# A hybrid retention and S5 layer on one Trainium2 core: S5 output loads on GpSimd's queue, grouped input statistics, and the first gate unit behind the chunk products

## The chip, the cores and the metric

The kernel runs on one core of one Trainium2 chip. Time is device time of one execution in microseconds (us), lower is better. The engines are named as the profile names them: PE (TensorE, matrix products), DVE (VectorE), ACT (ScalarE), POOL (GpSimd) and SP (SyncE, which here only issues DMAs). A DMA is issued by an engine's instruction stream and waits there for what it needs, so each of these streams is also a queue: a DMA that waits holds up all that is issued behind it on the same engine.

## What is computed

One layer of a hybrid backbone on 128 context tokens and 1024 latent tokens of width 1024, all in float32:

```
mod = silu(cond) @ w_ada + b_ada;  sh1, sc1, g1, sh2, sc2, g2 = split(mod)
h = norm(x) * (1 + sc1) + sh1
q, k, v, g, u = split(h @ w_in)
o = norm(retention(q, k, v)) * silu(g)            # 4 heads, both directions, chunks of 64
y = gelu(S5(u));  y = y * sigmoid(y @ w_glu + b_glu)   # 32 groups of 16 channels, 64 complex states
x = LN1(alpha * x + g1 * (concat(o, y) @ w_out))
f = relu(norm-modulated(x) @ w_ff1 + b_ff1)**2 @ w_ff2 + b_ff2
x = LN2(alpha * x + g2 * f)
```

The final retention and S5 states of the context tokens are outputs too.

## The kernel before

Tokens lie in 9 tiles of 128 rows (one of context, eight of latent tokens), taken in three groups of 384 (g = 0, 1, 2). An fp32 product is made of three matmuls on split operands (`mm3`, L206 to L210): `split` (L195) makes a high part on ACT or DVE (L200 or L198) and a low part on DVE or, with the mark "p", on POOL (L201). The program is one stream per engine, in the order in which the code emits it; all weights come through SP's queue with `ld`, a few loads and stores through POOL's queue with `gl`. Some 30 SBUF tiles are handed out in turn (`slot`, `rel`).

The order of the work around the change is this:

1. **Start.** The first round of modulation (`mod_begin(0)`, weights `wa`), the input normalisation `ln0` (L520) of the nine tiles, one tile at a time (statistics on DVE, a square root on ACT, the scaled copy on ACT, L523), and the S5 parameter tables: `params_a` (its last part on POOL, L404 to L417, and PE transposes, L421), `params_b` (powers, POOL, L438 to L443), `params_y` (POOL, L459 to L464).
2. **Products of the S5 input.** `make_h(g, k)` transposes a 128-column slice of the group on PE (L529), modulates it on ACT (L540) and splits it on DVE (L543); `products(g, k, k + 1)` then multiplies it with the first three S5 input columns (`u_split(0)` to `u_split(2)` are their splits). Group 2's normalisations are emitted among the steps of groups 0 and 1.
3. **Chunk products.** For each S5 column u, `s5_T1(u)` (DVE, L619 to L621) makes a table, `s5_W1(u)` transposes it (PE L635, copies on ACT L636), `load_X(u)` reads the column's inputs (SP, L602), and `s5_V(u)` multiplies (PE L649). Passes of input column 3 (`unit_g(3, g)`) and of column 4, the first gate (`unit_g(4, g)`), stand between them. A pass is 24 matmuls of 384 columns.
4. **Weave.** `weave` (L100, called in L1126) merges four tracks by costs that the code states: the other input columns (`units(5, 20)`), the scan and the tables for the outputs, a round of modulation, and `y_track(2)`, the S5 outputs of columns 0 and 1.
5. **Retention and the rest of S5.** `y_load(2)`, the heads' scores, `mod_more(2)` (modulation weights `wa`, SP, L259; products `pm`, PE L269), `s5_y(2)`, `y_load(3)`, `s5_y(3)`, then the gated unit (GLU), the output product and the feed-forward.

An S5 output u is `y_load(u)` and `s5_y(u)`: the load brings 3.3 MB from DRAM (KD in 8 pieces of 64 KB, X with 576 KB, and for each direction WD with 512 KB and SD with 576 KB) on SP's queue into three "vec" tiles, one "wide" tile and two held ones; PE makes 24 groups of products (`py`, L1102 to L1104), ACT the gelu, and POOL's queue stores the result to DRAM (YD, L1108) and reads it back in 8 pieces in another layout (yT, L1113). The next column's load goes into the same tiles, so it starts when this column's products are done, and its X waits for the store.

POOL also makes the query factors of the retention heads (`qf`, `qb`, L1182 and L1183), 128x1024 each.

Of the kernel before, what the change touches and what calls it, by code (L numbers as in the profile page):

```python
# [18 lines left out]
D = 1024  # L19
# [12 lines left out]
def kernel(  # L32
# [191 lines left out]
    xt = {}  # L224
# [204 lines left out]
    def params_b():  # L429
        e = PO.tensor_tensor  # L430

        def cmul(k0, k1, m):
            w = k1 - k0
            o0, o1 = Ar[:, k0:k1], Ai[:, k0:k1]
            x0, x1 = Ar[:, 1:1 + w], Ai[:, 1:1 + w]
            mr, mi = bc(Ar[:, m], 1, w), bc(Ai[:, m], 1, w)
            tv = tmpq.rearrange("p (k c) -> p k c", c=64)[:, 0:w]
            e(o0, x0, mr, MUL)  # L438
            e(tv, x1, mi, MUL)
            e(o0, o0, tv, SUB)  # L440
# [6 lines left out]
        cmul(5, 9, 4)  # L447

    def params_y():
# [397 lines left out]
    X4 = [load_X(u) for u in range(3)]
    u_load(4)
    run(back)
    unit_g(3, 0, evac_u(3))  # L850
    u_split(4, "p")
    s5_W1(0)
    run(s5_T1(1))
# [13 lines left out]
    unit_g(4, 1, evacs[4])  # L867
    load_outparams()
    s5_V(2, X4[2])
    s5_W1(3)  # L870
    unit_g(4, 2, evacs[4])
    u_split(5, "p")
    s5_V(3, X4[3])
    u_load(6)
    params_d()

    extra, UV = [0.0], 0
# [194 lines left out]
        return t  # L1072

    def y_load(u):
        if not late:
            s5s.close()
            late.append(late_s.enter_context(tc.tile_pool(name="late", bufs=1)))
        W3 = ltile()
        W3v = W3.rearrange("p (g x) -> p g x", g=8)
        for j in range(8):  # L1080
            ld(W3v[16 * j:16 * j + 16], KD[u, :, :, (7 - j) * 16:(7 - j) * 16 + 128].rearrange("g c x -> c g x"))
        X = hold(6) if u < NY else slot("yX")
        load_X(u, X)
        W2, SS = [], []
        for d in range(2):
            w, s = ltile(), ((hold(7) if u < NY else slot("yS")) if d == 0 else ltile(True))
            ld(w.rearrange("p (g n) -> p g n", g=8), WD[u, d].rearrange("p (g n) -> p g n", g=8)[:, :, 16 - 16 * d:144 - 16 * d])
            ld(s.rearrange("p (a n) -> p a n", a=2), SD[d, :, :, 4 * u:4 * u + 4].rearrange("p a q n -> p a (q n)"))
            W2.append(w.rearrange("p (g n) -> p g n", g=8))
            SS.append(s.rearrange("p (g n) -> p g n", g=8))  # L1090
            if d == 0:
                s0 = s
        YL[u] = W3v, X, W2, SS, s0

    def s5_y(u):
        W3v, X, W2, SS, s0 = YL.pop(u)
# [12 lines left out]
        if u >= NY:  # L1109
            rel(X, s0)  # L1110
# [52 lines left out]
    def ret_tok(h):  # L1163
        r = RS[h]
        qT, kT, vT = (qkv[h, w] for w in range(3))
        r["Sf"], r["Sb"], r["kb"] = slot("Sf"), slot("Sb"), slot("kb")
        ld(r["Sf"][:, 0:128], state_ret[0, 0, 0, h])
        ld(r["Sb"][:, 7 * P:8 * P], state_ret[0, 0, 1, h])
        kf, kb, vt = kT, r["kb"], vT
        for c0, c1 in batches:  # L1170
            n = (c1 - c0) * P
            pk, pv = ps("pk"), ps("pv")
            for c in range(c0, c1):
                PE.transpose(blk(pk, c - c0, c - c0 + 1), blk(kT, c, c + 1), ident)
# [5 lines left out]
        r["qf"] = hold(6 + h % 2)  # L1180
# [32 lines left out]
    def ret_out(h, now=True):  # L1213
# [531 lines left out]
```

## Time and profile before

| | us |
|---|---|
| median of 3 runs (lowest, highest) | 1504.29 (1502.57, 1504.37) |
| the profiled execution | 1499.46 |
| its span | 1497.2 |
| PE busy in the span | 1374.8 |
| DVE, ACT, POOL busy | 814.1, 599.6, 211.7 |

The profiled execution lies 4.8 us (0.3%) under the median of the runs, and 2.3 us of it lie outside the span. The profile gives for each engine what it did and what released it when it had waited; a busy PE counts as busy at either clock, so the granted clock is read beside it.

### The profile page before, as it was taken

What the parts mean: (1) busy time and instruction counts of PE and PEld (TensorE: products, weight loads), DVE (VectorE), ACT (ScalarE), POOL (GpSimd) and SP (SyncE); (2) the same over time, 40 slices, a digit from 0 to 9 for tenths busy, and PEclk for the clock granted to TensorE, in tenths of its full rate; (3) what the DMA queues carried; (4) which work ended last, traced back from release to release, by engine and by line L of the source; (5) the groups of instructions that cost most, each with busy time, mean ns of one, the idle gap of its engine ahead of it and who ended that gap; (6) DMA issues with size and microseconds to landing.
All of it is one profiled execution on the core that took longest, in us unless ns stands there. A gap on an engine that the chain in (4) does not pass through costs nothing.

```text
span 1497.2 us, 19638 instructions
## 1 busy us (share of the span) xinstructions
PE 1374.8 (92%) x7631; PEld 1233.0 (82%) x7631; DVE 814.1 (54%) x1486; ACT 599.6 (40%) x1001; POOL 211.7 (14%) x206
## 2 busy tenths in 40 slices
PE   5767999998658899999999999999999999999996
PEld 2557979998556788888999999989999999899995
DVE  7553689858315577676435443664544356543345
ACT  4453612122122463235444454444455444444451
POOL 3610000002141631253000010010001001000002
PEclk9888999999879989999999999999999999999998
DMA  9403561176578615138544334347443424734321
GB/s 319 107 1 123 167 223 59 43 192 189 153 213 246 199 47 181 64 122 261 198 132 152 118 110 138 108 135 239 143 126 111 128 98 141 253 114 140 115 83 43
DMA packets 194941, 214.62 MB, mean 143 GB/s; under 512 B 19800, under 2 KB 158752, under 8 KB 194336
## 3 DMA queue, kind: packets, MB, share of 16 engines
q1 hardware_dynamic: 186400, 197.99, 42.1%
q0 software_dynamic: 3504, 10.54, 2.4%
q10 hardware_dynamic: 4944, 4.83, 0.9%
q8 instruction: 60, 0.98, 0.3%
q14 instruction: 33, 0.27, 0.1%
HBM read 186.31 MB, written 27.02 MB: 142 GB/s over the span
## 4 chain that ended last, share of the span: by engine, by line
PE 71%; DVE 10%; DMA 6%; issue 5%; ACT 3%; SPq 3%; POOL 1%; POOLq 0%; ACTq 0%; DVEq 0%
PE ff L210 8%; PE ff L208 8%; PE ff L209 8%; PE acc L1575 8%; PE acc L1574 8%; PE acc L1573 8%; PE pu L208 4%; PE pu L209 3%; PE pu L210 3%; PE op L1427 2%; PE op L1426 2%; PE op L1428 2%; PE pv L649 1%; DMA w1r<-in_w_ff_dram 1%; PE pm L269 1%
## 5 line engine op out<-in xcount | busy, mean ns | idle before, releaser
L208 PE MATMUL ff<-h,wh 128*128 128x384 f32 x768 | 258.9, 337 | 0.0
L210 PE MATMUL ff<-h,wl 128*128 128x384 f32 x768 | 257.8, 336 | 0.7 <-DVE wl L201 0.7
L209 PE MATMUL ff<-h,wh 128*128 128x384 f32 x768 | 257.3, 335 | 0.0
L201 DVE TENSOR_TENSOR hid<-r,hid 128x384 fp32r<-128x384 f32 x96 | 67.5, 704 | 342.7 <-ACT hid L200 342.2
L1575 PE MATMUL acc<-wh,hid 128*128 128x512 f32 x564 | 222.4, 394 | 5.5 <-DVE hid L201 5.5
L1574 PE MATMUL acc<-wl,hid 128*128 128x512 f32 x564 | 221.7, 393 | 0.0
L1573 PE MATMUL acc<-wh,hid 128*128 128x512 f32 x564 | 220.1, 390 | 0.4 <-ACT hid L200 0.3
L1551 ACT ACTIVATE r<-ff,bf 128x384 f32<-128x384 f32 x96 | 55.6, 579 | 306.1 <-PE ff L210 306.0
L208 PE MATMUL pu<-hTh,wh 128*128 128x384 f32 x480 | 168.8, 352 | 1.9 <-DVE hTh L542 1.2
L209 PE MATMUL pu<-hTl,wh 128*128 128x384 f32 x480 | 165.5, 345 | 3.4 <-DVE hTl L543 3.3
L210 PE MATMUL pu<-hTh,wl 128*128 128x384 f32 x480 | 164.0, 342 | 0.0
L201 DVE TENSOR_TENSOR wl<-w1r,wh 128x1024 fp32r<-128x1024 f32 x96 | 117.5, 1224 | 60.7 <-ACT wh L200 56.1
L208 PEld LDWEIGHTS ff<-h,wh 128*128 128x128 f32 x768 | 144.2, 188 | 3.3 <-ACT wh L200 0.4
L209 PEld LDWEIGHTS ff<-h,wh 128*128 128x128 f32 x768 | 144.2, 188 | 2.9
L210 PEld LDWEIGHTS ff<-h,wl 128*128 128x128 f32 x768 | 144.1, 188 | 1.0 <-DVE wl L201 1.0
L1575 PEld LDWEIGHTS acc<-wh,hid 128*128 128x128 f32 x564 | 106.1, 188 | 29.5 <-DVE hid L201 7.2
L1573 PEld LDWEIGHTS acc<-wh,hid 128*128 128x128 f32 x564 | 106.4, 189 | 21.0 <-ACT hid L200 1.0
L1574 PEld LDWEIGHTS acc<-wl,hid 128*128 128x128 f32 x564 | 106.2, 188 | 20.5
L201 DVE TENSOR_TENSOR wl<-w2r,wh 128x1024 fp32r<-128x1024 f32 x95 | 118.0, 1242 | 0.9 <-PE acc L1575 0.6
L200 ACT ACTIVATE wh<-w1r 128x1024 fp32r<-128x1024 f32 x96 | 100.5, 1047 | 26.9 <-DMA w1r<-in_w_ff_dram 26.4
L208 PEld LDWEIGHTS pu<-hTh,wh 128*128 128x128 f32 x480 | 92.9, 193 | 11.6 <-issue 6.9
L200 ACT ACTIVATE wh<-w2r 128x1024 fp32r<-128x1024 f32 x96 | 100.3, 1045 | 0.0
(445 smaller groups left out, 2087.3 us busy)
## 6 DMA issues: line engine op xcount, KB each, us to landing
w1r<-in_w_ff_dram SPq DMA_DIRECT2D x96, 512.0 KB
w2r<-in_w_ff_dram SPq DMA_DIRECT2D x96, 512.0 KB
wa<-in_w_ada_dram SPq DMA_DIRECT2D x48, 512.0 KB
wr<-in_w_in_dram SPq DMA_DIRECT2D x20, 512.0 KB
SD<-SB SPq DMA_DIRECT2D x8, 576.0 KB
WD<-W SPq DMA_DIRECT2D x8, 576.0 KB
RD<-xr POOLq DMA_DIRECT2D x9, 512.0 KB, 2.9
x<-RD SPq DMA_DIRECT2D x9, 512.0 KB
```

What stands on the lines that cost most here:

```text
L200: S.activation(hi, x, AF.Copy)
L201: (tt if leng == "v" else PO.tensor_tensor)(lo, x, hi.bitcast(F32), SUB)
L208: PE.matmul(out, lhsT=wh, rhs=xh, start=first, stop=False)
L209: PE.matmul(out, lhsT=wh, rhs=xl, start=False, stop=False)
L210: PE.matmul(out, lhsT=wl, rhs=xh, start=False, stop=last)
L1426: PE.matmul(po[hf], lhsT=mh, rhs=wo[kt][0][:, cs], start=(kt == 0), stop=False)
L1427: PE.matmul(po[hf], lhsT=mh, rhs=wo[kt][1][:, cs], start=False, stop=False)
L1428: PE.matmul(po[hf], lhsT=ml, rhs=wo[kt][0][:, cs], start=False, stop=(kt == KT - 1))
L1551: S.activation(r, pu[:, 0:384], AF.Relu, bias=bf1[:, f:f + 1])
L1573: PE.matmul(o, lhsT=hh[:, 0, tk], rhs=wh[:, cs], start=(f == 0), stop=False)
L1574: PE.matmul(o, lhsT=hh[:, 0, tk], rhs=wl[:, cs], start=False, stop=False)
L1575: PE.matmul(o, lhsT=hh[:, 1, tk], rhs=wh[:, cs], start=False, stop=(f == NF - 1))
```

## The change

- The normalisation of x is made for three tiles at once: `ln0_stats(g)` takes the statistics of a group (the inverse root by iterations on DVE, for group 2 on POOL) and `ln0_norm(g)` the three scaled copies on ACT. They are emitted earlier than the single ones.
- The low parts of S5 columns 0 and 1 move from DVE to POOL; the last part of `params_a` is emitted behind them.
- `params_y` moves from POOL to DVE, in four pieces of three operations, emitted one by one among the later steps of the products, ahead of `s5_T1(0)`. Its sign change (B2) moves to POOL, into `params_b`.
- The chunk products are written in another order, with T1 and W1 of the next column further ahead of V, and without the first gate: `units(4, 20)` now has its three passes, in the weave.
- `y_load` issues on POOL's queue. `y_load(2)` is emitted at the end of the weave's track, behind `s5_y(1)`, and `y_load(3)`, into tiles of its own, ahead of the first head's scores.
- The query factors of heads 0 and 1 move from POOL to DVE.

```diff
-    def ln0(sl):
-        x = xt[sl][:, 0:D]
-        nb, rs = row_norm(x)
-        S.activation(x, x, AF.Identity, bias=nb[:, 0:1], scale=rs[:, 0:1])
+    def ln0_stats(g, eng=None):
+        mv, rs = row_stats([xt[sl] for sl in range(3 * g, 3 * g + 3)], eng)
+        lnp[g] = neg_mean(mv, rs, 3, eng), rs
+
+    def ln0_norm(g):
+        nb, rs = lnp.pop(g)
+        for i in range(3):
+            x = xt[3 * g + i][:, 0:D]
+            S.activation(x, x, AF.Identity, bias=nb[:, i:i + 1], scale=rs[:, i:i + 1])
...
-            e = PO.tensor_tensor
-            e(y1, B1, q_r, MUL)
-            e(tv, B2, q_i, MUL)
-            e(y1, y1, tv, ADD)
+            tt(y1, B1, q_r, MUL)
+            tt(tv, B2, q_i, MUL)
+            tt(y1, y1, tv, ADD)
+            yield
...
-    for sl in range(3):
-        ln0(sl)
-    next(pa)
-    u_split(0)
+    ln0_stats(0)
+    ln0_norm(0)
+    u_split(0, "p")
...
-    u_split(1)
+    u_split(1, "p")
     u_split(2, "p")
+    ln0_stats(1)
+    ln0_norm(1)
+    next(pa)
...
-    back = s5_T1(0)
+    back = chain(params_y(), s5_T1(0))
...
-        if (g, k) in ((0, 5), (0, 7), (1, 5)):
-            ln0(6 + ((0, 5), (0, 7), (1, 5)).index((g, k)))
-        if g == 2 and k < 4:
-            next(back)
+        if (g, k) == (0, 7):
+            ln0_norm(2)
+        if (g, k) == (1, 4):
+            u_split(3, "p")
+        if j >= 4:
+            next(back, None)
         products(g, k, k + 1)
...
-    unit_g(4, 0, evacs[4])
-    s5_V(1, X4[1])
+    load_outparams()
     s5_W1(2)
     run(s5_T1(3))
+    s5_V(1, X4[1])
+    X4.append(load_X(3))
+    u_split(4, "p")
...
+        own = u == 3
+        vt = (lambda: slot("yv")) if own else ltile
+        W3 = vt()
+        X = slot("yX") if own else hold(6)
...
-            ld(W3v[16 * j:16 * j + 16], KD[u, :, :, (7 - j) * 16:(7 - j) * 16 + 128].rearrange("g c x -> c g x"))
-        X = hold(6) if u < NY else slot("yX")
-        load_X(u, X)
+            gl(W3v[16 * j:16 * j + 16], KD[u, :, :, (7 - j) * 16:(7 - j) * 16 + 128].rearrange("g c x -> c g x"))
+        gl(X, XD[u].rearrange("j (c g) n -> (j c) (g n)", g=8))
...
-    weave(units(5, 20), chain(s5_scan(), spill(), s5_w2(), tables()), mod_round(2, 5.0, 5.0, 2), chain(s5_finish(), y_track(NY)))
+    weave(units(4, 20), chain(s5_scan(), spill(), s5_w2(), tables()), mod_round(2, 5.0, 5.0, 2), chain(s5_finish(), y_track()))
...
-        PO.tensor_tensor(v8(r["qf"]), v8(qT), bc(RT[:, h], 1, 8), MUL)
-        PO.tensor_tensor(v8(qT), v8(qT), bc(RT[:, 4 + h], 1, 8), MUL)
+        e(v8(r["qf"]), v8(qT), bc(RT[:, h], 1, 8), MUL)
+        e(v8(qT), v8(qT), bc(RT[:, 4 + h], 1, 8), MUL)
...
-    y_load(2)
+    y_load(3)
     ret_scores(0)
...
     s5_y(2)
-    y_load(3)
```

**PE's order in the chunk products.** A row is the place of an instruction in PE's stream, its line, operation, output and inputs; pu is the output of a pass of an input column, pw that of `s5_W1`, pv that of `s5_V`, and wh_636 and wh_749 hold column 3, wh_1067 and wh_1327 the first gate. Before:

```order
314 L210 MATMUL pu_1115<-hTh_698,wl_637 128x384
315 L649 MATMUL pv_1141<-X_1030,W_211_1071 64x144 x4
...
322 L649 MATMUL pv_1190<-X_1030,W_214_1084 64x144 x4
323 L208 MATMUL pu_1197<-hTh_350,wh_636 128x384
...
346 L210 MATMUL pu_1197<-hTh_698,wl_637 128x384
347 L635 MATMUL pw_1225<-ident_71,T_217_1097 128x128 x4
...
350 L635 MATMUL pw_1244<-ident_71,T_220_1106 128x128 x4
351 L208 MATMUL pu_1272<-hTh_350,wh_1067 128x384
...
374 L210 MATMUL pu_1272<-hTh_698,wl_1068 128x384
375 L649 MATMUL pv_1299<-X_1032,W_233_1224 64x144 x4
```

After:

```order
314 L210 MATMUL pu_1059<-hTh_677,wl_750 128x384
315 L644 MATMUL pw_1086<-ident_71,T_174_984 128x128 x4
...
342 L210 MATMUL pu_1129<-hTh_677,wl_750 128x384
343 L658 MATMUL pv_1156<-X_980,W_182_1031 64x144 x4
...
350 L658 MATMUL pv_1205<-X_980,W_185_1044 64x144 x4
351 L644 MATMUL pw_1226<-ident_71,T_197_1111 128x128 x4
...
354 L644 MATMUL pw_1245<-ident_71,T_200_1120 128x128 x4
355 L658 MATMUL pv_1269<-X_982,W_191_1085 64x144 x4
...
383 L658 MATMUL pv_1503<-X_1325,W_250_1441 64x144 x4
384 L507 MATMUL ps_1510<-ident_71,cst_1216 128x128
...
391 L508 MATMUL ps_1528<-ident_71,cst_1216 128x128
392 L208 MATMUL pu_1552<-hTh_319,wh_1327 128x384
```

V of column 0 stood behind the second pass of column 3 and one W1, with gate passes between the V's; now it stands behind the third pass and two W1, a W1 stands between two V's, and the gate's first pass follows the last of the chunk products.

**POOL's queue at the end of the weave.** late, ub, yv, yX and yS are tiles that `y_load` fills; YD and yT are the stores and the reads back of `s5_y`. Before:

```order
76 L974 DMA RTd<-qd_3390 8x128
77 L975 DMA RT_1677<-RTd 128x1024
78 L1108 DMA YD<-ub_396_2705 128x8x144
79 L1113 DMA yT_3549<-YD 16x8x144 x8
80 L1108 DMA YD<-ub_396_2705 128x8x144
81 L1113 DMA yT_3633<-YD 16x8x144 x8
82 L1132 DMA bgl_3642<-in_b_glu_dram 128x4x1
```

After:

```order
88 L1118 DMA YD<-ub_376_2700 128x8x144
89 L1122 DMA yT_3420<-YD 16x8x144 x8
90 L1092 DMA late_3429<-KD 16x8x128 x8
91 L1093 DMA ub_376_2700<-XD 128x1152
92 L1099 DMA late_3439<-WD 128x8x128
93 L1100 DMA ub_376_2700<-SD 128x2x576
94 L1099 DMA late_3442<-WD 128x8x128
95 L1100 DMA late_3443<-SD 128x2x576
...
97 L1122 DMA yT_3583<-YD 16x8x144 x8
98 L1092 DMA late_3592<-KD 16x8x128 x8
...
104 L1141 DMA bgl_3609<-in_b_glu_dram 128x4x1
105 L1092 DMA yv_3611<-KD 16x8x128 x8
```

The six kinds of load of a column now stand between the reads back of the column before (yT) and the column's own store (YD); column 2's load and column 3's, into tiles of its own, stand behind yT of column 1.

**SP's queue from the last input column on.** wr is a weight column, Sf and Sb the retention's first states, wa the modulation's weights. Before:

```order
96 L1081 DMA late_3558<-KD 16x8x128 x8
...
98 L1087 DMA late_3568<-WD 128x8x128
99 L1088 DMA ub_396_2705<-SD 128x2x576
...
102 L1081 DMA late_3644<-KD 16x8x128 x8
103 L602 DMA yX_3653<-XD 128x1152
104 L1087 DMA late_3655<-WD 128x8x128
...
108 L1167 DMA Sf_3679<-in_state_ret_dram 128x128
...
111 L1168 DMA Sb_3736<-in_state_ret_dram 128x128
112 L259 DMA wa_3776<-in_w_ada_dram 128x1024
113 L259 DMA wa_3778<-in_w_ada_dram 128x1024
```

After:

```order
88 L1048 DMA KD<-Kp_3098 16x2x240 x4
89 L314 DMA wr_3177<-in_w_in_dram 128x8x128
90 L1176 DMA Sf_3646<-in_state_ret_dram 128x128
91 L1177 DMA Sb_3647<-in_state_ret_dram 128x128
92 L1176 DMA Sf_3703<-in_state_ret_dram 128x128
93 L1177 DMA Sb_3704<-in_state_ret_dram 128x128
94 L259 DMA wa_3745<-in_w_ada_dram 128x1024
95 L259 DMA wa_3747<-in_w_ada_dram 128x1024
```

SP's queue goes from the last weight column to Sf, Sb and the modulation's weights, with no load of an S5 output ahead of them.

## Rows read from the trace of the kernel before

**Rows 1.** the page, part 4: shares of the span in the chain of waits, by engine.

```profile
PE 71%; DVE 10%; DMA 6%; issue 5%; ACT 3%; SPq 3%; POOL 1%; POOLq 0%; ACTq 0%; DVEq 0%
```

**Rows 2.** waits of PE, 0 to 180 us (released line <- releaser: total us, times, longest).

```profile
PE xt L529 <- ACT xb L523: 14.9, 4, 7.9
...
PE pv L649 <- ACT W L636: 7.9, 1, 7.9
PE xt L529 <- ACT hTh L540: 5.5, 1, 5.5
...
PE pu L209 <- DVE hTl L543: 3.3, 7, 1.1
```

**Rows 3.** waits of PE, 320 to 580 us.

```profile
PE pm L269 <- DMA wa<-in_w_ada_dram: 20.7, 2, 15.1
PE py L1103 <- DMA ub<-SD: 7.2, 1, 7.2
```

**Rows 4.** windows (length, busy time and count by engine, granted clock, DMA share, GB/s).

```profile
75.00:100.00 25.00, 11.48 (x45) 10.73 (x46) 10.46 (x28) 12.54 (x26) 4.25 (x4) 0.73 0.00 1
...
358.00:385.00 27.00, 27.00 (x154) 26.77 (x147) 22.76 (x91) 4.37 (x12) 2.33 (x6) 0.94 0.56 171
400.00:450.00 50.00, 24.24 (x159) 20.76 (x160) 4.78 (x13) 10.67 (x21) 16.57 (x17) 0.67 0.80 214
```

**Rows 5.** PE's timeline, 97 to 127 us (start, length, instruction, idle time before it).

```profile
97.15 0.52 PE L210 MATMUL pu<-hTh,wl 128*128 128x384 f32 x1
97.47 0.52 PE L208 MATMUL pu<-hTh,wh 128*128 128x384 f32 x1
...
126.49 0.33 PE L208 MATMUL pu<-hTh,wh 128*128 128x384 f32 x1
126.67 0.33 PE L209 MATMUL pu<-hTl,wh 128*128 128x384 f32 x1
```

**Rows 6.** DVE's timeline, 70 to 105 us.

```profile
71.58 1.53 DVE L543 TENSOR_TENSOR hTl<-h,hTh 128x384 fp32r<-128x384 f32 x1
...
103.67 0.56 DVE L543 TENSOR_TENSOR hTl<-h,hTh 128x384 fp32r<-128x384 f32 x1 [2.58 <-ACT hTh L540]
104.14 0.69 DVE L619 TENSOR_TENSOR T<-Ar,Y 128x512 f32<-128x512 f32 x1
```

**Rows 7.** POOL's timeline, 34 to 69 us.

```profile
34.60 3.80 POOL L201 TENSOR_TENSOR wl<-wr,wh 128x512 fp32r<-128x512 f32 x2 [2.04 <-ACT wh L200]
...
67.38 1.49 POOL L464 TENSOR_TENSOR Y<-Y,pY 128x512 f32<-128x512 f32 x1
```

**Rows 8.** PE's timeline, 390 to 452 us.

```profile
390.99 0.34 PE L209 MATMUL pu<-hTl,wh 128*128 128x384 f32 x1
...
394.81 0.34 PE L210 MATMUL pu<-hTh,wl 128*128 128x384 f32 x1
...
419.74 2.17 PE L1158 MATMUL psc<-qkv,qkv 128*128 128x128 f32 x18
...
450.19 0.41 PE L1102 MATMUL py<-yX,late 128*128 128x144 f32 x2
```

**Rows 9.** POOL's timeline, 378 to 402 us (issues of DMAs).

```profile
378.72 0.58 POOL L975 DMA_DIRECT2D RT<-RTd  x1 [4.67 <-DMA RTd<-qd]
392.06 0.93 POOL L1108 DMA_DIRECT2D YD<-ub  x1 [12.76 <-ACT ub L1106]
397.14 4.22 POOL L1113 DMA_DIRECT2D yT<-YD  x8 [4.15 <-DMA late<-KD]
```

**Rows 10.** DMA issues of POOL, 385 to 470 us (KB each, median us from issue to landing).

```profile
yT<-YD POOLq DMA_DIRECT2D x24, 72.0 KB, 7.2
YD<-ub POOLq DMA_DIRECT2D x2, 576.0 KB, 4.4
```

**Rows 11.** SP's queue, 419 to 442 us (issues of DMAs).

```profile
419.44 4.32 SPq L1081 DMA_DIRECT2D late<-KD  x8
...
433.14 8.86 SPq L259 DMA_DIRECT2D wa<-in_w_ada_dram  x6
```

More of the change, by code (lines that the diff above doesn't have):

```diff
@@ L447, in params_b @@
         cmul(5, 9, 4)
+        B2 = s5in["B"][0:64, 512:1024]
+        PO.tensor_scalar(B2, B2, -1.0, None, MUL)
     def params_y():
@@ L798 @@
         make_h(0, k)
-    u_split(1)
+    u_split(1, "p")
     u_split(2, "p")
+    ln0_stats(1)
+    ln0_norm(1)
+    next(pa)
     for u in range(NU):
         products(0, 0, 4, (u,))
-    for sl in range(3, 6):
-        ln0(sl)
+    make_h(1, 0)
+    make_h(1, 1)
     run(pa)
     params_b()
-    make_h(1, 0)
-    make_h(1, 1)
     products(1, 0, 1)
@@ L818 @@
     next(steps)
+    ln0_stats(2, PO)
     products(1, 2, 3)
@@ L821 @@
     del waA, waB
-    params_y()
-    u_split(3, "p")
     order = [(g, k) for g in range(2) for k in range(4, KT)] + [(2, k) for k in range(KT)]
@@ L833 @@
     products(1, 3, 4)
-    back = s5_T1(0)
+    back = chain(params_y(), s5_T1(0))
     for j, (g, k) in enumerate(order):
         ahead(j + 3)
-        if (g, k) in ((0, 5), (0, 7), (1, 5)):
-            ln0(6 + ((0, 5), (0, 7), (1, 5)).index((g, k)))
-        if g == 2 and k < 4:
-            next(back)
+        if (g, k) == (0, 7):
[4 more added lines that the diff above has]
+            next(back, None)
         products(g, k, k + 1)
+    run(back)
     for u in range(NU):
         rel(*uw[u])
+    u_load(4)
+    X4 = [load_X(u) for u in range(2)]
+    run(s5_T1(1))
+    unit_g(3, 0, evac_u(3))
+    s5_W1(0)
     SB = big("SB")[:, 0:64 * NCOL].rearrange("p (r d l n) -> p r d l n", r=2, d=2, l=16)
@@ L846 @@
     SE = SE_.rearrange("p (r d l s) -> p r d l s", r=2, d=2, l=16)
[L847 to L853, printed above, removed]
     unit_g(3, 1, evac_u(3))
-    s5_V(0, X4[0])
-    unit_g(3, 2, evac_u(3))
     s5_W1(1)
     run(s5_T1(2))
-    X4.append(load_X(3))
+    unit_g(3, 2, evac_u(3))
+    s5_V(0, X4[0])
+    X4.append(load_X(2))
     u_load(5)
-    unit_g(4, 0, evacs[4])
-    s5_V(1, X4[1])
+    load_outparams()
     s5_W1(2)
     run(s5_T1(3))
+    s5_V(1, X4[1])
+    X4.append(load_X(3))
+    u_split(4, "p")
     params_s()
     params_c()
-    unit_g(4, 1, evacs[4])
-    load_outparams()
     s5_V(2, X4[2])
     s5_W1(3)
-    unit_g(4, 2, evacs[4])
-    u_split(5, "p")
     s5_V(3, X4[3])
-    u_load(6)
     params_d()
@@ L1077, in y_load @@
             late.append(late_s.enter_context(tc.tile_pool(name="late", bufs=1)))
-        W3 = ltile()
-        W3v = W3.rearrange("p (g x) -> p g x", g=8)
+        own = u == 3
+        vt = (lambda: slot("yv")) if own else ltile
+        W3 = vt()
+        X = slot("yX") if own else hold(6)
+        tiles = [W3, X]
+        W3v = W3[:, 0:D].rearrange("p (g x) -> p g x", g=8)
         for j in range(8):
-            ld(W3v[16 * j:16 * j + 16], KD[u, :, :, (7 - j) * 16:(7 - j) * 16 + 128].rearrange("g c x -> c g x"))
-        X = hold(6) if u < NY else slot("yX")
-        load_X(u, X)
+            gl(W3v[16 * j:16 * j + 16], KD[u, :, :, (7 - j) * 16:(7 - j) * 16 + 128].rearrange("g c x -> c g x"))
+        gl(X, XD[u].rearrange("j (c g) n -> (j c) (g n)", g=8))
         W2, SS = [], []
         for d in range(2):
[L1086 to L1089, printed above, removed]
+            w, s = vt(), slot("yS") if own else hold(7) if d == 0 else ltile(True)
+            tiles += [w, s]
+            wv = w[:, 0:D].rearrange("p (g n) -> p g n", g=8)
+            gl(wv, WD[u, d].rearrange("p (g n) -> p g n", g=8)[:, :, 16 - 16 * d:144 - 16 * d])
+            gl(s.rearrange("p (a n) -> p a n", a=2), SD[d, :, :, 4 * u:4 * u + 4].rearrange("p a q n -> p a (q n)"))
+            W2.append(wv)
             SS.append(s.rearrange("p (g n) -> p g n", g=8))
-            if d == 0:
-                s0 = s
-        YL[u] = W3v, X, W2, SS, s0
+        YL[u] = W3v, X, W2, SS, tiles if own else []
     def s5_y(u):
-        W3v, X, W2, SS, s0 = YL.pop(u)
+        W3v, X, W2, SS, tiles = YL.pop(u)
         Xv = X.rearrange("p (g n) -> p g n", g=8)
@@ L1108, in s5_y @@
         gl(YD[u].rearrange("g p n -> p g n"), Xv)
-        if u >= NY:
-            rel(X, s0)
+        rel(*tiles)
         yt = ltile(True) if u == 3 else slot("yT")
@@ L1115, in s5_y, with y_track @@
         dump(f"yT{u}", yt)
-    def y_track(n):
-        for u in range(n):
+    def y_track():
+        for u in range(2):
             y_load(u)
-            yield YL1
+            yield 22.0
             s5_y(u)
             extra[0] += 5.5
-            yield YL2
-    YL1, YL2, NY = 22.0, 2.0, 2
-    weave(units(5, 20), chain(s5_scan(), spill(), s5_w2(), tables()), mod_round(2, 5.0, 5.0, 2), chain(s5_finish(), y_track(NY)))
+            yield 2.0
+        y_load(2)
+    weave(units(4, 20), chain(s5_scan(), spill(), s5_w2(), tables()), mod_round(2, 5.0, 5.0, 2), chain(s5_finish(), y_track()))
     rel(*hTh, *hTl)
@@ L1179, in ret_tok @@
             S.copy(blk(vt, c0, c1), pv[:, 0:n])
-        r["qf"] = hold(6 + h % 2)
+        r["qf"] = slot("qf") if h < 2 else hold(6 + h % 2)
+        e = tt if h < 2 else PO.tensor_tensor
         v8 = lambda z: z[:, 128:1152].rearrange("p (c i) -> p c i", c=8)
-        PO.tensor_tensor(v8(r["qf"]), v8(qT), bc(RT[:, h], 1, 8), MUL)
-        PO.tensor_tensor(v8(qT), v8(qT), bc(RT[:, 4 + h], 1, 8), MUL)
+        e(v8(r["qf"]), v8(qT), bc(RT[:, h], 1, 8), MUL)
+        e(v8(qT), v8(qT), bc(RT[:, 4 + h], 1, 8), MUL)
     def ret_kv(h):
@@ L1235, in ret_out @@
         if h < 2:
-            rel(qb, vt)
+            rel(qb, vt, qf)
         if now:
```

9 lines of the change are left out of this document (5 added, 4 removed).

## The prediction

> **What bounds the kernel now.** PE carries 71% of the chain of waits [rows 1], and the change leaves its matmuls as they are, so the time can fall only where PE stands idle or runs at the lower clock. I read the waits of PE next, in two stretches that hold what the diff touches. Up to 180 us [rows 2] the longest are transposes that wait for a normalised tile (14.9 us in four waits, the longest 7.9), a transpose behind ACT's hTh (5.5), V of column 0 behind W (7.9), and products behind the low part hTl (3.3 in seven). From 320 us on [rows 3] it is modulation products behind their weights (20.7 in two, the longest 15.1), and the S5 output products behind SD (7.2). The windows [rows 4] show what idling costs besides: from 75 to 100 us PE was busy for 11.5 of 25 us at a mean granted clock of 0.73, from 400 to 450 us for 24.2 of 50 at 0.67. At the upper level (2.4 GHz) matmuls follow each other every 0.17 to 0.18 us, at the lower (1.2 GHz), just after such a wait, every 0.32 [rows 5]. What follows 580 us is not touched and shifts as a whole.
>
> **Part 1, start and products of the S5 input.** Minus is faster.
>
> - The 7.9 and the 5.5 us [rows 2] come from one cause: group 2's tiles are normalised one by one, DVE, ACT, DVE, ACT, behind each other's queues. With the statistics of three tiles made before the group is due, both go: -13.4. The other three waits of that row (14.9 - 7.9 = 7.0) are for group 1's tiles, whose statistics also come earlier, but PE's L421 transposes and DVE's other work stand near; I take -1.5 (ends 0 and -7).
> - The hTl of 71.58 us took 1.53 us while POOL was still at `params_y` (1.49 an operation); alone it took 0.56 [rows 6, 7]. With those operations gone from POOL, the 3.3 us of hTl waits go: -3.
> - Added: `params_y` on DVE, 12 operations of the size and kind of T1's, 0.69 each [rows 6], three to a step, plus the step's hTl of 0.56: 2.6 us, where PE's step takes about 1.9 (estimate: nine matmuls at 0.174 and three transposes). Four steps make +2.9. `u_split(3)` on POOL then slows DVE once more, I take +2. Sum +5; ends 0 (DVE runs ahead by the steps buffered) and +10 (each of the eight steps slowed by POOL).
> - Two more low parts on POOL, 3.80 us each [rows 7]: they stand ahead of products that are not due for 5 us or more, and beside `params_a`, which nothing needs before the T1 tables. Nothing; without that cover up to 4, within the +10 above.
>
> **Part 2, chunk products.** The 7.9 us for W vanish, since in the new order V of column 0 stands behind two W1 and the third pass: -7.9. New tightness: W1 and V of the next columns follow each other without gate passes between, and column 2's X is loaded into a tile just freed. No row shows these waits; the nearest is the 7.9 for W itself, the other end is nothing. I take +4 (ends 0, +9). The three gate passes leave: the 22 intervals between the second and the last of a pass's 24 matmuls take 3.82 us (390.99 to 394.81 [rows 8]), so a pass takes 4.17 and three make -12.5 here.
>
> **The clock.** Behind each of the three long waits PE works at the lower level for a while. From the mean clock of 0.73, 13.5 of those 25 us were at the lower level [rows 4]; taking 4 us of work behind each wait, that costs 2 us each: -6 (ends -3, -8).
>
> Parts 1, 2 and the clock without the passes: -13.4 - 1.5 - 3 + 5 - 7.9 + 4 - 6 = -22.8 (ends about -30 and -12). The weave then begins 35 us earlier. By the order it has 38 passes up to its last chunk kernel (pK) in both kernels, the gate's three now at the head, and ten behind that place instead of seven; PE is full in it, so I let it shift unchanged. `params_s`, `params_c`, the query factors on DVE and the sign change on POOL stand beside that work: nothing; without cover 2 us.
>
> **Part 3, the S5 outputs.** Counted on before's clock, from the end of y(0)'s products (390.8, just ahead of the pass of [rows 8]). Before, the store is issued at 392.06 (0.93 us) and the eight reads back from 397.14 to 401.36 [rows 9]; y(1) ended at 419.74 and y(2) began at 450.19 [rows 8]. PE now has four passes there instead of one: 16.7 us, which take the place of waiting, so the 12.5 us moved are hidden if y(1) comes no earlier. y(1)'s loads now stand behind the eight reads back on POOL, and a queue lets no more than eight DMAs be under way: KD from 401.4 to 405.6 at the earliest, or 3 us later if each waits for a read back to land (7.2 us [rows 10]); then X, two WD (as the store, 0.93 each) and two SD (0.6 each, as RT's 0.58 [rows 9]): 3.7 us more, 409 to 412. Landing takes 4.4 (store) to 7.2 (reads back), and the modulation's weights share the engines: y(1) starts at 414 to 422, I take 422, and ends at 429.5, 10 us later than before.
>
> Between y(1) and y(2) PE had 15.3 us of work and 15.1 of waiting for weights (30.45 in all [rows 3, 8]). The weights leave SP 8.9 us of issues [rows 11] that stood behind column 2's load, issued from 419.44; now nothing holds them, so that wait goes. In its place y(2) waits for its own load: store at 430.5, reads back to 440, loads to 448 or 451, landed at 456: +6 against 450.2 (ends -5, where only PE's work counts, and +14). y(3)'s load, into its own tiles, follows at once, two heads' products ahead of its use: nothing; without that cover it would be what y(2) pays, 6. The second wait for weights (20.7 - 15.1 = 5.6) goes, as SP is no longer held up by column 3's load: -5.5 (ends 0 and -5.6).
>
> **Sum.** -22.8 - 12.5 + 6 - 5.5 = -34.8 on the profiled 1499.5: 1464.7. That execution lay 4.8 under its median; I add half of that, as the next one need not: **1467**. Own range of this case: 1457 to 1478.
>
> **The rivals.**
>
> 1. *Loads on POOL and weights on SP meet.* y(1)'s load (3.3 MB), column 0's reads back (0.6) and six modulation weights (3.1) now want the DMA engines from about 405 us on. At the 214 GB/s of the window 400 to 450 [rows 4] 7 MB take 33 us, so y(1) would start at 433 to 438 and y(2) at 464 to 470: 14 to 20 us instead of 6, and more if lanes also wait. Time 1476 to 1488, I take 1480. For it: that window's DMA share was 0.80 with PE half idle. Against: it is a mean over idle stretches. The Trainium skill ("DMA: Bandwidth & Descriptors", Issuing engines are not separate DMA queues) says that DMAs of all issuing engines run on the same 16 DMA engines, so another queue saves only issue time; by it the weights gain the 13.7 us of issues that stood ahead of them (419.44 to 433.14 [rows 11]) and no transfer gets shorter. No run here shows the two at once. Chance 0.2.
> 2. *The front stays bound.* DVE, with `params_y` and POOL's splits beside it, sets the pace in the products, and the chunk products wait for W: part 1 and 2 at their other end, -12. Time 1478, up to 1488 with a late y(1). Chance 0.08.
> 3. *Slower: a column's load takes much longer on POOL.* Its WD and KD are 512-byte pieces, 1024 in a WD. y(1) and y(2) have no time to spare, y(0) a little, which I leave out. If each load takes L longer, the loss is 3L, and it eats the 35 us from L = 12; at 20 us the time is 1467 + 60 = 1527. For it: the reads back, 72 KB each, took 7.2 us to land [rows 10]; no row shows such a load there. Against: the store of 1024 pieces took 0.93 us to issue and 4.4 to land, and RT's issue 0.58 us in a stretch where DVE was busy for 22.8 of 27 us [rows 4, 9]. The Trainium skill (same page, SWDGE vs HWDGE vs iDMA) says that GpSimd writes the descriptors of its DMAs into SBUF, from which some DVE work locks it out; RT's row does not show that. Chance 0.07.
> 4. *No change.* The shift of 23 us before the weave is waited for inside it (weight columns on SP), and y(2) costs what the passes gave. Time 1500 to 1506. Against: PE is full in the weave. Chance 0.04.
> 5. *Better.* Part 1 at its low end and y(2) as early as PE's work allows: 1450. Chance 0.03.
>
> **The numbers.** The forecast gets 0.58. A measurement here tells 0.2%, 3 us, from no change. Faster: 0.58 + 0.2 + 0.08 + 0.03 = 0.89; same 0.04; slower 0.07. The range reaches over rivals 1 and 2, 1457 to 1488, and leaves out 0.14 and the tails.
>
> **What would show it.** Right: no wait over 3 us of PE before the weave but the first ones, its beginning at 140 to 144 us; no wait for W; y(1) some 30 us behind y(0) with four passes in between, a wait of 8 to 14 us for SD or WD ahead of y(2), none for modulation weights. Wrong: T1 or hTl ahead of PE for more than 10 us, y loads that land over 15 us after their issue, or PE waiting inside the weave where before it did not.

## The result, and the profile after

The changed kernel takes 1464.55 us (median of 4 runs, 1460.46 to 1465.77) against 1503.43 (4 runs of the kernel before, same chip): ratio 0.9738, 95% interval 0.9716 to 0.976, so 38.9 us faster. The profiled execution took 1460.46 us, with a span of 1458.4, 38.8 less than before's.

Where the span went is read from the same events in both timelines of PE:

| event | before | after | difference | since the event above |
|---|---|---|---|---|
| first pass of the weave | 177.35 | 138.56 | -38.8 | -38.8 |
| first product of y(0) | 384.94 | 342.60 | -42.3 | -3.6 |
| first work behind y(1) | 419.74 | 384.44 | -35.3 | +7.0 |
| first work behind y(2) | 456.07 | 420.88 | -35.2 | +0.1 |
| first product of y(3) | 486.97 | 443.63 | -43.3 | -8.1 |
| end of the span | 1497.2 | 1458.4 | -38.8 | +4.5 |

The waits of PE up to 180 us, to be held against [rows 2]:

```profile
PE xt L538 <- ACT xb L532: 5.4, 3, 3.9
...
PE pu L209 <- DVE hTl L552: 3.0, 3, 2.2
PE pu L208 <- ACT hTh L549: 1.8, 1, 1.8
```

The three waits for group 1's tiles are still there (14.9 less 7.9 was 7.0, now 5.4); those for a tile of group 2 (7.9), for hTh (5.5) and for W (7.9) are gone. Two windows show what is left, the products of groups 1 and 2, and the chunk products:

```profile
75.00:100.00 25.00, 21.80 (x105) 20.18 (x106) 20.04 (x34) 15.21 (x24) 3.02 (x2) 0.80 0.00 1
105.00:138.50 33.50, 33.36 (x379) 31.75 (x378) 24.92 (x71) 25.35 (x88) 2.58 (x1) 1.00 0.71 206
```

In the first PE is busy for 21.8 of 25 us, where it was busy for 11.5 [rows 4], still at a mean clock of 0.80; in the second it works for 33.36 of 33.50 us at the full clock, so the chunk products in their new order have no wait left. The timeline of PE from y(0) to y(2) (the last field is the idle time before a row and what ended it):

```profile
368.15 0.48 PE L1112 MATMUL py<-ub,late 128*128 128x144 f32 x2 [2.87 <-issue]
371.28 0.82 PE L1113 MATMUL py<-ub,late 128*128 128x144 f32 x2 [2.64 <-DMA ub<-SD]
377.60 0.82 PE L1114 MATMUL py<-late,late 128*128 128x144 f32 x2 [5.50 <-DMA late<-SD]
...
384.44 2.17 PE L1167 MATMUL psc<-qkv,qkv 128*128 128x128 f32 x18
...
405.01 0.82 PE L1112 MATMUL py<-ub,late 128*128 128x144 f32 x2 [7.70 <-DMA ub<-XD]
408.37 0.82 PE L1113 MATMUL py<-ub,late 128*128 128x144 f32 x2 [2.54 <-DMA ub<-SD]
412.98 0.82 PE L1114 MATMUL py<-late,late 128*128 128x144 f32 x2 [3.79 <-DMA late<-SD]
```

y(1) has waited 2.9 + 2.6 + 5.5 = 11.0 us and y(2) 7.7 + 2.5 + 3.8 = 14.0, both for loads (for the 2.9 the profile names no releaser; X, issued at 362.71, landed in 5.0 us in the median, which is about then); no wait of the modulation products is among the rows from 280 us on. That list has a new one, for the query factors of head 2:

```profile
PE py L1114 <- DMA late<-SD: 9.3, 2, 5.5
PE py L1112 <- DMA ub<-XD: 7.7, 1, 7.7
PE po L1236 <- POOL ub L1192: 5.3, 1, 5.3
...
PE po L1237 <- POOL ub L1193: 1.6, 1, 1.6
```

POOL's queue shows what stands ahead of the loads and of the factors (issues of DMAs, with the idle time before them):

```profile
349.72 0.92 POOL L1118 DMA_DIRECT2D YD<-ub  x1 [11.46 <-ACT ub L1116]
354.33 4.22 POOL L1122 DMA_DIRECT2D yT<-YD  x8 [3.69 <-DMA YD<-ub]
358.54 4.18 POOL L1092 DMA_DIRECT2D late<-KD  x8
...
365.79 0.71 POOL L1100 DMA_DIRECT2D late<-SD  x1
...
461.71 4.21 POOL L1122 DMA_DIRECT2D late<-YD  x8 [9.96 <-DMA YD<-yX]
465.94 2.35 POOL L1192 TENSOR_TENSOR ub<-ub,RT 128x1024 f32<-128x1024 f32 x1
```

The load of column 1 is issued behind the eight reads back of column 0: its last part at 365.79, 16.1 us behind the store at 349.72. The eight reads back of column 3 wait 10 us for their store to land, and the factors for head 2, next on POOL, come only at 465.94. In the kernel before, these factors stood behind the same reads back, but the reads back waited 3.7 us:

```profile
494.15 0.93 POOL L1108 DMA_DIRECT2D YD<-yX  x1 [3.63 <-ACT yX L1106]
498.76 4.21 POOL L1113 DMA_DIRECT2D late<-YD  x8 [3.68 <-DMA YD<-yX]
502.99 2.40 POOL L1182 TENSOR_TENSOR ub<-ub,RT 128x1024 f32<-128x1024 f32 x1
```

What differs is the traffic beside the store. Before, SP's next load (the gate, GD) waited for that store to land:

```profile
SPq L1217 <- DMA YD<-yX: 9.3, 1, 9.3
```

In the changed kernel, where column 3's load has other tiles, this wait is gone: SP issues the gate at 450.10 and three loads of 512 KB up to 451.46, beside the store of 450.82. From 451 to 456 us the DMA engines moved 319 GB/s, against 135 before between the store and its landing (494.5 to 499).

### The profile page after: what moved, and what is told of

It is laid out like the page before. It is cut to its first block, busy times and chain, and to the rows that moved or that the text cites. A ratio compares the mean times of both kernels' runs of the same rounds, so it can differ in the third digit from the quotient of the medians.

```text
span 1458.4 us, 19628 instructions
## 1 busy us (share of the span) xinstructions
PE 1367.7 (94%) x7631; PEld 1230.0 (84%) x7631; DVE 809.2 (55%) x1473; ACT 595.0 (41%) x990; POOL 227.4 (16%) x260
## 4 chain that ended last, share of the span: by engine, by line
PE 50%; DVE 9%; issue 3%; ACT 3%; DMA 2%; POOL 1%; POOLq 0%; SPq 0%; DVEq 0%; ACTq 0%
PE ff L210 8%; PE ff L208 8%; PE ff L209 8%; PE acc L1584 8%; PE acc L1583 8%; PE acc L1582 8%; DMA w1r<-in_w_ff_dram 1%; DVE xr L1449 1%; DVE st L157 1%; DVE op L1448 1%; DVE st L158 1%; DVE o L1627 1%; DVE hid L201 1%; ACT xr L1454 1%; DMA RD<-xr 0%
## 5 line engine op out<-in xcount | busy, mean ns | idle before, releaser
L1582 PEld LDWEIGHTS acc<-wh,hid 128*128 128x128 f32 x564 | 106.4, 189 | 21.8 <-ACT hid L200 1.8
```

The costliest lines, as they stand in the source:

```text
L1582: PE.matmul(o, lhsT=hh[:, 0, tk], rhs=wh[:, cs], start=(f == 0), stop=False)
```

## The experiments

Each is compared with the kernel before by its ratio; a difference of ratios times 1500 us gives the distance from the changed kernel (0.9738). With the intervals of both ratios its bounds are about 4 us.

| run | edit of the changed kernel | median | ratio (95%) | against the change, us |
|---|---|---|---|---|
| e1 | loads of S5 outputs on SP | 1472.98 | 0.9799 (0.9783 to 0.9814) | +9 |
| e2 | first gate among the chunk products | 1491.26 | 0.9919 (0.9902 to 0.9935) | +27 |
| e3 | group 2 normalised tile by tile | 1473.45 | 0.9807 (0.9792 to 0.9821) | +10 |
| e4 | reads back behind the next load | 1449.47 | 0.9646 (0.9628 to 0.9664) | -14 |
| e5 | all query factors on DVE | 1454.53 | 0.9691 (0.9677 to 0.9706) | -7 |
| e6 | temporary of `params_y` in its own tile | 1465.2 | 0.9762 (0.9748 to 0.9775) | +4 |
| e7 | e4, e5 and e6 together | 1438.84 | 0.9588 (0.957 to 0.9605) | -22 |
| e8 | `params_y` on POOL | 1458.87 | 0.9712 (0.9696 to 0.9727) | -4 |
| e9 | before, with the S5 output part alone | 1509.94 | 1.0053 (1.0039 to 1.0067) | |
| e10 | e7 and two more | 1437.31 | 0.9576 (0.9559 to 0.9594) | -24 |
| e11 | e4, e5 and e8 together | 1433.08 | 0.9547 (0.9533 to 0.9561) | -29 |

**e1, the loads on SP.**

```diff
-            gl(W3v[16 * j:16 * j + 16], KD[u, ...
+            ld(W3v[16 * j:16 * j + 16], KD[u, ...
```

and likewise for X, WD and SD.

> The changed kernel with the loads of all four S5 outputs back on SP's queue, at the new places in the program. Theory (on POOL the load of a column is behind the eight reads back of the column before, 8 to 9 us; on SP it is ahead of the modulation's weights): PE's wait before y(1) falls from 11.0 us by 5 to 8, y(2) starts up to 5 us earlier against y(1), and the wait for modulation weights, which the change removed, returns with 10 to 20 us, since y_load(2) and y_load(3) now both stand ahead of them; in all 2 to 15 us slower than the changed kernel (1467 to 1480). Rival (only the DMA engines' rate counts, the queue does not matter): within 3 us of the changed kernel, y(1) and y(2) at the same distances from y(0).

The waits of PE from 200 us on:

```profile
PE pm L269 <- DMA wa<-in_w_ada_dram: 28.2, 1, 28.2
...
PE py L1114 <- DMA late<-SD: 3.6, 1, 3.6
...
PE py L1113 <- DMA ub<-SD: 1.3, 1, 1.3
```

y(1) waits 4.9 us instead of 11.0, and the wait for modulation weights is back, 28.2 us, more than expected: SP's queue issued the weights at 410.55, behind both loads. The rival, that the queue doesn't matter, falls: inside the change, the move to POOL trades one queue's order for another's and is worth 9 us. What it is worth without the rest, e9 tells.

**e2, the gate passes back in front.**

```diff
+    unit_g(4, 0, evacs[4])
     params_s()
     params_c()
+    unit_g(4, 1, evacs[4])
     s5_V(2, X4[2])
     s5_W1(3)
+    unit_g(4, 2, evacs[4])
+    u_split(5, "p")
     s5_V(3, X4[3])
+    u_load(6)
...
-    weave(units(4, 20), ...
+    weave(units(5, 20), ...
```

> The changed kernel with the three passes of the first gate back among the chunk products. Theory (they fill a wait whose end the loads set): the weave begins 12.5 us later, PE's wait before y(1) grows from 11.0 to some 23.5 us, and the time rises by 12 to 14 us (1476 to 1479). Rival (the passes cost the same everywhere, the loads would have come earlier without them): the wait stays at 11 us and the time within 3 us of the changed kernel.

The time rose by 27 us, twice what I expected. In the profiled executions, 18.9 stand before the weave (its first pass at 157.5, not 138.6): the passes' 12.5, and 6.4 of which 3.6 are PE's waits for column 4's split (1.5 for ACT's part, 2.1 for POOL's). 4.1 stand in the weave, and 5.5 between y(0) and the end of y(1), though three passes less stand there: y(1)'s wait grew from 11.0 to 27.3 us. POOL's queue behind y(0) in this run:

```profile
372.73 0.92 POOL L1123 DMA_DIRECT2D YD<-ub  x1 [13.34 <-ACT ub L1121]
377.59 4.22 POOL L1127 DMA_DIRECT2D yT<-YD  x8 [3.95 <-DMA YD<-ub]
384.82 1.18 POOL L1097 DMA_DIRECT2D late<-KD  x2 [3.01 <-DMA yT<-YD]
...
396.57 0.71 POOL L1105 DMA_DIRECT2D late<-SD  x1
```

```profile
376.22 3.21 SPq L259 DMA_DIRECT2D wa<-in_w_ada_dram  x6
```

With one pass behind y(0) instead of four, the last tiles that the passes hold come free earlier, and the six modulation weights go out at 376.22, just ahead of the reads back at 377.59. These land late, and KD, which needs their places in the queue, waits: the last part of the load is issued 23.8 us behind the store instead of 16.1. So the passes do two things: they fill the wait, and they keep the weights out of the reads back's way. The second I had not seen; it is read from this trace, and in e9, again with one pass, y(1)'s longest wait is the same 21.6 us.

**e3, group 2 tile by tile.**

```diff
-    ln0_stats(2, PO)
...
-        if (g, k) == (0, 7):
-            ln0_norm(2)
+        if (g, k) in ((0, 5), (0, 7), (1, 5)):
+            ln0(6 + ((0, 5), (0, 7), (1, 5)).index((g, k)))
```

> The changed kernel with the normalisation of group 2 as before, tile by tile with a square root on ACT, at its old places. Theory (the waits of 7.9 and 5.5 us and the clock after them came from these): waits of 10 to 15 us return in the products, products end 12 to 18 us later, time 1476 to 1483. Rival (the new order of the tables and the splits removed them, or DVE with params_y is late anyway): under 5 us slower.

```profile
PE xt L543 <- ACT xb L527: 12.1, 1, 12.1
...
PE xt L543 <- ACT ub L594: 2.5, 1, 2.5
PE xt L543 <- ACT hTh L554: 2.0, 1, 2.0
```

16.6 us of waits return: 12.1 + 2.5 at the first transposes of group 2, and 2.0 at a transpose of group 1, behind ACT, which stands at group 2's first tile. The time rises by 10: a little less than I gave, as the waits of some 4 us that the changed kernel has for hTl and hTh at this place lie under them. The 12.1 are longer than the 7.9 of before because the last tile's statistics here also stand behind the first piece of `params_y` on DVE (79.98 to 84.96 us). The cause of the two waits of before is shown.

**e4, the reads back behind the next load.**

```diff
             y_load(u)
+            if u:
+                y_back(u - 1)
             yield 22.0
             s5_y(u)
...
         y_load(2)
+        y_back(1)
```

`y_back` is the part of `s5_y` that reads YD into yT; for columns 2 and 3 it is called right behind `s5_y`, as before.

> The changed kernel with the eight reads back of a column behind the next column's load on POOL's queue. Theory (the queue's serial order sets y(1) and y(2)): each load is issued some 8 us earlier, PE's waits of 11.0 us before y(1) and 14.0 before y(2) fall to 0 to 4 and 4 to 8, time 12 to 20 us under the changed kernel (1445 to 1453). Rival (the DMA engines' rate, shared with the modulation's weights and the reads back, sets them): the waits shrink by under 3 us each, time 1459 to 1465.

```profile
353.54 0.92 POOL L1118 DMA_DIRECT2D YD<-ub  x1 [12.46 <-ACT ub L1116]
354.45 4.24 POOL L1092 DMA_DIRECT2D late<-KD  x8
...
361.88 0.71 POOL L1100 DMA_DIRECT2D late<-SD  x1
362.57 2.12 POOL L1124 DMA_DIRECT2D yT<-YD  x4
```

```profile
371.68 0.48 PE L1114 MATMUL py<-late,late 128*128 128x144 f32 x2 [2.09 <-DMA late<-SD]
...
391.77 0.48 PE L1112 MATMUL py<-ub,late 128*128 128x144 f32 x2 [1.75 <-issue]
396.20 0.82 PE L1113 MATMUL py<-ub,late 128*128 128x144 f32 x2 [3.95 <-DMA ub<-SD]
401.08 0.82 PE L1114 MATMUL py<-late,late 128*128 128x144 f32 x2 [4.07 <-DMA late<-SD]
```

The load's last part is issued 8.3 us behind the store, not 16.1; y(1) waits 2.1 us and y(2) 9.8. The time falls by 14 us, as the theory of the serial queue says; the wait before y(2) is longer than I gave.

**e5, all query factors on DVE.** The edit is `e = tt` for every head.

> The changed kernel with the query factors of heads 2 and 3 on DVE too. Theory (the new waits of PE for them, 5.3 and 1.6 us, come from their place on POOL behind the reads back of y(3), which wait 10 us for its store): both waits go, 5 to 7 us faster than the changed kernel (1457 to 1460). Rival (what stands behind the waits, the scores of the next head on ACT or the loads, is late as well): under 2 us.

Both waits for the factors are gone from the list, and the time falls by 7 us, the 5.3 and 1.6 of them.

**e6, the temporary in its own tile.** In the changed kernel DVE stood still for 2.9 us in the middle of `params_y`:

```profile
75.64 0.69 DVE L459 TENSOR_TENSOR Y<-pB,pq 128x512 f32<-128x512 f32 x1
79.24 0.69 DVE L460 TENSOR_TENSOR pY<-pB,pq 128x512 f32<-128x512 f32 x1 [2.92 <-POOL wl L201]
...
80.58 0.55 DVE L552 TENSOR_TENSOR hTl<-h,hTh 128x384 fp32r<-128x384 f32 x1
```

The tile of the temporary had been handed out from the weight column that POOL's `u_split(3)` was still reading.

```diff
-        sY, sB12 = slot("pY"), s5in["B"]
+        sY, sB12 = t512("pY"), s5in["B"]
```

> The changed kernel with the temporary of params_y in a small tile of its own and not in one of the tiles handed out in turn. Theory (DVE's wait of 2.9 us at 76 us is for the tile that POOL's low part of column 3 still reads): it goes, and PE's wait of 2.2 us for hTl with it, 2 to 4 us faster (1460 to 1463). Rival (POOL's splits hold DVE off in themselves): DVE's operations get longer instead, no change within 1.5 us.

```profile
76.45 2.05 DVE L460 TENSOR_TENSOR pY<-pB,pq 128x512 f32<-128x512 f32 x1
78.53 1.89 DVE L461 TENSOR_TENSOR Y<-Y,pY 128x512 f32<-128x512 f32 x1
80.34 0.55 DVE L552 TENSOR_TENSOR hTl<-h,hTh 128x384 fp32r<-128x384 f32 x1
```

The rival is right: without the wait, DVE's operations beside POOL's split take 2.05 and 1.89 us instead of 0.69, and hTl comes at 80.34 instead of 80.58. The kernel is no faster, if anything slower.

**e7, the three together.**

> The three edits of e4, e5 and e6 together. Theory (three different waits on PE's path): the gains add, 1434 to 1446. Rival (what one frees is waited for at the next): not faster than the best of the three alone by more than 3 us.

The gains of e4 and e5 add (14 + 7 against 22): the waits were separate.

**e8, `params_y` on POOL.** The code of before, run behind `run(steps)`, with the T1 steps from j = 8.

> The changed kernel with params_y back on POOL at its old place, the rest as changed. Theory (on DVE it costs little, on POOL it makes hTl of group 0's and 1's later steps late): hTl waits of 2 to 4 us return about 60 to 72 us, the wait of 2.2 us at 81 us and the tight steps behind it go; within 3 us of the changed kernel either way. Rival (POOL now also has the splits and params_a, so params_y ends late and the T1 tables with it): 5 to 12 us slower.

Its products end at 101.2 instead of 105.4, and the time falls by 4 us, at the edge of what I gave. hTl beside POOL's operations takes longer, as in [rows 6]:

```profile
65.20 1.30 DVE L552 TENSOR_TENSOR hTl<-h,hTh 128x384 fp32r<-128x384 f32 x1
66.87 1.20 DVE L552 TENSOR_TENSOR hTl<-h,hTh 128x384 fp32r<-128x384 f32 x1 [0.37 <-ACT hTh L549]
```

but PE does not wait for these: its waits for hTl are 0.8 and 0.5 us, at 76 and 79 us. POOL, which makes group 2's inverse root first, comes to `params_y` at 63.9 us, when DVE has three of group 0's four later steps split, and the rest is made far enough ahead. The lower clock that follows the changed kernel's wait at 81 us is gone with it: the mean granted clock of 60 to 138 us is 1.00.

**e9, the S5 output part alone, on the kernel before.** Loads on POOL at the new places, query factors of heads 0 and 1 on DVE, start and chunk products as before; the edit is the part of the change's diff from `y_load` on, with `units(5, 20)`.

> The kernel before with only the S5 output part of the change: loads on POOL's queue at the new places, query factors of heads 0 and 1 on DVE; start, statistics and chunk products as before, one pass between y(0) and y(1). Theory (the queue alone does not pay, the three passes and the front do): the waits for modulation weights, 20.7 us in two, go, but y(1) waits some 27 us and y(2) 14, as in the run with the gate among the chunk products, and PE waits 5 to 7 for the query factors; 2 to 10 us slower than before (1503 to 1511 by its clock). Rival (the queue move is a gain of its own, of the size of the waits it removes): 6 to 15 us faster than before.

```profile
PE py L1106 <- DMA ub<-XD: 30.1, 2, 21.6
PE py L1107 <- DMA ub<-SD: 6.4, 2, 3.8
...
PE py L1108 <- DMA late<-SD: 5.4, 2, 3.0
PE po L1230 <- POOL ub L1186: 4.5, 1, 4.5
```

It is 0.5% slower than before: the 20.7 us for weights [rows 3] are gone, but y(1) and y(2) wait 42 us for loads, and PE 6.4 for the factors. Alone, this part of the change, the queue move with its new places, is a loss.

**e10, two more edits on e7.** The low part of column 3 on DVE (`u_split(3)`), and WD and SD of y(1) with `ld`.

> The kernel with all three edits, and two more: the low part of column 3 on DVE, and WD and SD of y(1) on SP's queue, which stands free there. Theory (DVE and POOL slow each other in that step, and y(1) waits for the last SD on POOL's queue): 2 to 4 us less in the products and 3 to 4 less before y(1), 5 to 8 us under it (1431 to 1434). Rival (DVE is the bound of that step whoever makes the low part, and the DMA engines set the landing): under 2 us.

No difference from e7 that the intervals tell (0.9576 and 0.9588), as the rival gave.

**e11, e4, e5 and e8 together.**

> The changed kernel with params_y on POOL (as in e8), the reads back behind the next load (as in e4) and all query factors on DVE (as in e5). Theory (three separate places on PE's path): 3 to 5 us under the kernel with all three earlier edits, 1433 to 1436. Rival (an earlier weave is waited for at y(1), whose loads are the next limit): within 1.5 us of it.

1433.08 us, ratio 0.9547: 4.5% faster than before, 2% faster than the change, and by the ratios 6 us under e7. It is the best version here; its list still has 12.9 us of waits of S5 output products (6.5 + 4.1 for loads, 2.3 with no releaser named).

## Why the prediction was right, and where its steps were not

The forecast was 1467 us with a sum of -34.8 on the profiled execution; measured were 1464.55 and -38.8 of span. Step by step:

- **Waits of group 2's tiles, -13.4.** Right, and e3 shows the cause. **Group 1's, -1.5:** 7.0 became 5.4, -1.6.
- **hTl, -3.** The waits were in the trace, and so was the slow hTl beside POOL, but the move to DVE was not what it took to end them. In e8 `params_y` on POOL slows hTl as before (1.30 us) and PE hardly waits for it, since POOL comes to it when DVE has three of the four steps split. And 3.0 us of hTl waits came back at other steps, 2.2 of them behind `params_y` on DVE. The term is about nothing.
- **`params_y` on DVE, +5.** Right in size: e8 is 4 us faster without it, with bounds of about 4. Part of it is POOL's split beside it, as I took it, though the form was first a wait for a tile and, with that removed (e6), the slowness itself.
- **W, -7.9,** right; **new waits in the chunk products, +4:** nothing. PE was busy for 33.36 of 33.50 us there.
- **The clock, -6.** Before, PE worked 5.2, 3.8 and 5.0 us at the lower level around and behind the three long waits, 14.0 in all where I took 12. One such stretch is left, behind the new wait for hTl, with 7.9 us of work. The first of the three before, and the one left:

```profile
78.70:85.50 6.80, 5.17 (x19) 5.08 (x20) 3.58 (x11) 3.43 (x7) 0.63 (x1) 0.52 0.00 0
76.70:86.80 10.10, 7.89 (x28) 7.26 (x27) 7.46 (x13) 7.33 (x12) 2.50 (x2) 0.50 0.01 2
```

A matmul of 384 columns takes 0.32 us at the lower level and 0.17 at the upper [rows 5], so about half of the work's time at the lower level is lost, and the clock gave back some 3 us (an estimate from these figures: half of 14.0 less half of 7.9).

- **The front** gave 26.3 us (38.8 less the 12.5 of the passes) and not 22.8. The waits for tiles and for W make 22.9 of it (13.4 + 1.6 + 7.9). The other four terms, hTl, `params_y`, the chunk products' waits and the clock, cancel in my sum (-3 + 5 + 4 - 6 = 0) and made -3.4, nearly all of it the clock. What `params_y` costs is within them, as the 3.0 us for hTl and the stretch at the lower level. The waits of the chunk products are the term that was too dear.
- **The weave unchanged.** It was 3.6 us shorter (384.94 - 177.35 = 207.6 against 342.60 - 138.56 = 204.0); with the passes in front again (e2) it took 208.1. 2.0 of it are waits ahead of pK (4.3 + 1.4 us in before's list, 3.7 in after's): PE was not quite full there, though I took it to be. The other 1.6 are the clock behind them: its mean from 358 to 385 us was 0.94 before [rows 4], which is 3.2 us at the lower level, and 1.00 over the whole weave after. Not forecast.
- **Passes, -12.5, hidden in the wait before y(1).** Right; e2 shows that the place is worth more than that: of its 27 us, 12.5 are the passes, 5.5 stand before the end of y(1), where the weights were no longer held back, and the rest in the chunk products and the weave. **y(1) 39 us behind y(0):** 36.1 (384.44 - 348.39, the end of y(0)'s products). The last part of the load was issued 17.4 us behind y(0)'s end, where I gave 18 to 21.
- **y(2), +6 against y(0).** Its products ended 72.5 us behind those of y(0) (420.88 - 348.39), against 65.4 before (456.07 - 390.72): +7.1. Right.
- **The second wait for weights, -5.5.** Gone: from the end of y(2) to y(3) the kernel gained 8.1: the wait's 5.5, and 2.6, most of it the lower clock behind it, which I had not counted. Before, the eight modulation products behind that wait took 3.19 us and the next eight 1.70; eight take 1.06 in the changed kernel. The mean granted clock of this stretch was 0.89 before and 1.00 after.
- **What I did not see** is the last row of the table: 4.5 us are given back after y(3). PE's waits for the query factors that stay on POOL grew from 1.2 to 6.9 us; e5, without them, gains 7. Their place behind the reads back of y(3) is the old one; the reads back come later, because the store ahead of them lands later. I took y(3)'s load into other tiles for free. Before, the gate load on SP waited for column 3's store, and with it what stands behind it there; with the new tiles it does not. In all twelve traces with these tiles the gate goes out within 1 us of that store and the reads back wait 6.7 to 10.3 us for it, with the loads on SP (e1) and without the new front (e9) too, so it is neither the queue nor the front. That it is the loads beside the store that slow it is read from the traces; no run holds them back alone.

That the sum came within 4 us is in part luck: the front, the weave and the second wait for weights gave 3.5, 3.6 and 2.6 us more than I had, and y(2) and what follows y(3) took 1.1 and 4.5 back.

Of the rivals, the meeting of loads and weights did not come in its size: y(1)'s last load was waited for until 29.2 us behind y(0)'s end (377.60), not 42 to 47. But e2 and e9 show it at work as soon as the passes don't hold the weights back, and the store of y(3) shows it in the changed kernel. The rule of the Trainium skill that I set beside it ("DMA: Bandwidth & Descriptors", Issuing engines are not separate DMA queues: another issuing engine saves only issue time) is not tested alone by these runs. On POOL a 512 KB part of a load landed 7.6 us after its issue and SD 7.0 to 9.7 (medians); PE went on 7.1 and 11.8 us after the issue of y(1)'s two SD, against 11.3 and 13.8 on SP in e1, where the reads back went out beside them. But the order within a queue was worth more than the issue time: 14 us by e4, for the same transfers. The front did not stay bound. Slow loads on POOL, the rival on the other side, would have needed 12 us more for each; their landing was within 3 us of what I took. The rule of the Trainium skill (the same title, SWDGE vs HWDGE vs iDMA) that some DVE work locks GpSimd out of writing descriptors was not tried alone: the issues of WD on POOL took 0.91 to 0.93 us in the changed kernel, as the store did before [rows 9].

## What to carry to other kernels

Before moving DMAs to a free queue, write down what stands ahead of them there and what that waits for: here the same loads cost 14 us or not by whether eight small reads back, which nobody needed soon, were issued ahead of them. A wait that the order of a queue sets can be filled with work taken from elsewhere, but then the work and the move must be judged together: the S5 output part alone was a loss of 0.5%, while inside the whole change its queue was worth 9 us. And when a wait of a queue goes, ask what it held back: here SP's next loads no longer waited for a store, went out beside it, and what stood behind that store on POOL had to wait 6 us longer for it.

## What the runs showed of the hardware that I had not expected

DVE and POOL slow each other, and DVE the more: POOL's two subtractions of 128x512 took 3.02 us in the changed kernel, with DVE standing still, and 3.48 beside a DVE multiplication and an addition of 128x512 in e6, which took 2.05 and 1.89 us instead of 0.69. Taking away a wait of DVE for POOL gained nothing, because the contention took the same time.

The eight reads back of 72 KB landed in 3.2 us (median) in the changed kernel, where SP's weights went out later, and in 7.2 before [rows 10], where a column's load went out beside them on SP's queue. The store of 576 KB took 4.0 us to land for the first columns (median) and 10.6 for column 3, beside which SP's loads went out.
